# Paired matmuls on the parts of the array: inner products, chunk outputs and first low-rank factors of an RWKV-7 scan

## The chip, the cores and the metric

The kernel runs on one core of one Trainium2 chip, in one launch. The metric is the device time in microseconds (us) of one execution. The core's engines each work through their own list of instructions in order: PE (TensorE, matrix products into PSUM), DVE (VectorE), ACT (ScalarE), POOL (GpSimd) and SP, which here only starts transfers (DMA). An instruction waits where data or a buffer of another engine isn't there yet, and everything behind it on its engine waits too.

## The reference, cut to what matters

A net of several blocks on 1024 tokens of 1024 features, float32. The change is in one of them, the RWKV-7 time mix with 16 heads of 64 features:

```python
xs = x[None] + xx[None] * mu[:, None, None, :]          # six token-shift mixes
xr, xw, xk, xv, xa, xg = xs
r, k, v = jnp.einsum('nbtd,nde->nbte', jnp.stack([xr, xk, xv]), w_rkv)
w = -jax.nn.softplus(-(w0 + jnp.tanh(xw @ w1) @ w2)) - 0.5
a = jax.nn.sigmoid(a0 + (xa @ a1) @ a2)
g = jax.nn.sigmoid(xg @ g1) @ g2
...
def step(S, inp):                                       # one token, all heads
    r_t, w_t, k_t, v_t, a_t, b_t = inp
    sa = jnp.einsum('bhvk,bhk->bhv', S, a_t)
    S = S * w_t[:, :, None, :] + sa[..., None] * b_t[:, :, None, :] + v_t[..., None] * k_t[:, :, None, :]
    y = jnp.einsum('bhvk,bhk->bhv', S, r_t)
    return S, y
```

`w1` and `a1` are 1024 x 64, `g1` is 1024 x 160. The blocks ahead of it (a recurrent mixer, an FFN, an embedding) and behind it (output projection, FFN, embedding, a second net) aren't touched.

## The kernel before, in words

The time mix has two parts that are woven together on all engines.

The **dense part** (`rwkv_dense`) goes over four segments of 256 tokens. A segment has 28 units; a unit is one PSUM tile `mm` and eight steps over the features, each taking one mixed input (`M`, in 13 slots) and one slice of a 128-column weight tile. First come 8 units for v, then the four first low-rank factors (`low`), then 8 for r and 8 for k. The r, k and v units take three matmuls per step on operands split in two (L249 to L251 in the helper `mm3`); the four low-rank ones take one plain float32 matmul (L885). `w1` and `a1` are loaded side by side as the columns 0 to 63 and 64 to 127 of one tile, `both`; the unit of mix 1 and the unit of mix 4 each load that tile, each multiply all 128 columns, and each keep only their own 64 rows of the result. Mixes are made by ACT and DVE, weights come by DMA from the ACT queue, and split weights take ACT (L861) and DVE (L863). `finish` makes the scan's operands of a segment, and a chunk of 64 tokens can enter the scan when its segment's are in DRAM.

The **scan** (`rwkv_scan`) goes over 16 chunks of 64 tokens; the two heads of a pair lie on partitions 0 to 63 and 64 to 127. For each chunk: `inner` makes the products inside the chunk (tile `AM`, three slots, so that chunk c waits for the output of chunk c - 3), four pairs at a time from one load `BK`; their diagonal blocks go through DRAM to DVE, which inverts them by substitution (L1146, L1149), and back (L1157, L1168); `chain` carries the state (L1244, L1247, L1255, L1264); `outs` makes the chunk's output y for four pairs at a time (L1289 with the state, L1291 with the chunk's own tokens); `post` normalizes. `rwkv_out` projects the outputs of chunks that are done (tile `XO`).

A planner, `weave_`, sets the order of the instructions on every engine before the launch: tasks are generators that yield steps with an engine, a duration, waits and PSUM banks, and it issues next the step that a rough clock of the engines would start first. The durations in the steps only set that order. PSUM has 3 banks for the tag `g` (inner products, second factors and small products), 2 for `mm`, 2 for `ch`, 1 for `y`.

A float32 matmul stands in the trace as two records, so 8 records are 4 matmuls. In `inner` a matmul has 64 rows and 128 columns of the array, in L1289 64 by 64, in L1291 128 by 64, and elsewhere mostly 128 by 128; the trace writes that in front of the operand (`64*128`).

Of the kernel before, what the change touches and what calls it, by code (L numbers as in the profile page):

```python
# [10 lines left out]
AF = mybir.ActivationFunctionType  # L11
# [3 lines left out]
P = 128  # L15
# [41 lines left out]
class Net:  # L57
    """Feature-major activations: tile [128 features, 512 tokens] per (k, half)."""
# [16 lines left out]
    def open_group(self, T, W, S, L, psum):  # L75
        """Pools of one part of the net: T and S slots of [128, 516], weight slots, PSUM banks per tag."""
        self.close_group()
        self.bigx = ExitStack()
        self.nT = T
        self.big = self.bigx.enter_context(self.tc.tile_pool(name="big", bufs=1, reuse_waits="tile"))  # L80
        self.open_work(W, S, L, psum)

    def open_work(self, W, S, L, psum):
        """All of them but T anew."""
# [8 lines left out]
    def open_top(self):  # L93
        """One more pool above the group's, closed before them."""
# [4 lines left out]
    def open_rtop(self):  # L99
        """Another one, from the other end of the memory."""  # L100
# [44 lines left out]
    def s(self, dt=F32, n=HT):  # L145
        """scratch [128, n <= 516]"""
# [3 lines left out]
    def extra(self, tag, shape, dt, every, bufs):  # L150
        """now and then a slot of the pool on the right, where that is for more of the others"""
# [7 lines left out]
    def ld(self, src=None, n=HT, rows=P):  # L159
        """tile for a load; loads have slots of their own, for they run ahead"""  # L160
# [66 lines left out]
    def load_ws(self, srcs, nk, m, tag="w"):  # L227
        """srcs: DRAM APs arranged [p, nk, n] for columns c..c+n; returns hi, lo tiles [P, nk, m]"""
# [17 lines left out]
    def mm3(self, ps, w, x, first, last):  # L246
        """ps += w.T @ x with w = (hi, lo), x = (hi, lo)"""
# [5 lines left out]
    # W columns [c0, c0+128) for all nk row tiles  # L253
# [3 lines left out]
    def lin(self, w, xs, nk):  # L257
        """xs: list of (hi, lo) per k -> PSUM tile"""
# [6 lines left out]
    def rstd_bcast(self, acc, scale, eps, acc2=None):  # L265
        """acc [128, 512] -> PSUM [128, 512]: (sum over partitions * scale + eps)^-0.5 on all partitions; with acc2,
        for which that is the factor of another norm: that one and the product of both"""
# [34 lines left out]
    def square(self, h, k, half, gain=None):  # L302
        """h[k][half] is final: its part of the sum of squares (and of that of the products with the gain)"""
# [60 lines left out]
    def blocks(self, nblk, units, in_unit, post, nk_out, wout, h, add_bias=None, lag=2, delay=3, mid=None, late=None, fill=None, nlate=LATE):  # L364
        """units: weight items per block; in_unit(b, i, half, w) ; post(b, half) -> list of nk_out (hi, lo)"""
# [51 lines left out]
        # the first half of the last block before the second half of the one before it  # L417
# [34 lines left out]
    def hawk(self, h, xn, mid, late):  # L452
# [5 lines left out]
        # c8 = 8 softplus(-lam), softplus(z) = max(z, 0) + log1p(exp(-|z|)), log1p(e) = 2 atanh(e / (2 + e))  # L458
# [100 lines left out]
    def ple_prep(self, layer):  # L559
        """p, features on the partitions, split"""  # L560
# [40 lines left out]
    NSEG, SN = 4, 256  # token segments of the dense part  # L601

    def rwkv_consts(self):
# [7 lines left out]
        # block-diagonal ones (2 heads), identity minus the same / 64, and per-head selector columns  # L611
# [8 lines left out]
        # [s, t] masks on both heads: s < t | s <= t  # L620
# [19 lines left out]
        # operands of the scan, one chunk of 64 tokens after another  # L640
        self.qD, self.bkD, self.gbD = (d((16, P, KD, 2, 64), nm) for nm in ("qD", "bkD", "gbD"))
        self.vD = d((16, P, KD, 64), "vD")
        # second factors of the low-rank parts, for one pair after another
# [5 lines left out]
        # per head pair the decays between chunk middles; at the segments' ends in two factors  # L649
# [1636 lines left out]
```

## Time and profile before

| | |
|---|---|
| runs | 4188.85 us median of 3 (4186.73, 4188.85, 4215.79) |
| profiled execution | span 4186.6 us from the first to the last instruction; the page gives no other time for it |
| PE busy | 3949.4 us, 94% of the span |
| DVE, ACT, POOL busy | 61%, 35%, 4% |
| mean granted TensorE clock | 0.957 |
| woven stretch, dense part and scan | about 1340 to 2400 us |

The span of the profiled execution is within 0.1 us of the fastest run, so sums against it are sums against the runs. A busy PE is not PE at its peak: its matmuls are pipelined, so what a group costs is read from the starts of neighbouring instructions, not from their durations. PEclk is the granted clock as a share of 2.4 GHz; 0.5 is 1.2 GHz.

### The profile page before, as it was taken

How to read it: one execution, taken by the hardware profiler on the slowest of the kernel's cores; microseconds unless marked ns; L12 is line 12 of the kernel's file. 1: busy time of each engine (PE TensorE's matmuls, PEld its weight loads, DVE VectorE, ACT ScalarE, POOL GpSimd, SP SyncE). 2: the span in 40 equal slices, each digit the busy share in tenths (PEclk: the TensorE clock that was granted, in tenths of full speed). 3: DMA queues.
4: the chain of work that ended last, by engine and by line, in shares of the span. 5: the costliest groups of instructions: out<-in, count | busy, mean ns of one | idle time of the engine just before them, and what ended most of it. 6: DMA issues, size and time to landing. Idle time of an engine off the chain costs nothing.

```text
span 4186.6 us, 58441 instructions
## 1 busy us (share of the span) xinstructions
PE 3949.4 (94%) x22510; PEld 3216.6 (77%) x22510; DVE 2544.7 (61%) x5192; ACT 1466.1 (35%) x2491; POOL 179.3 (4%) x376
## 2 busy tenths in 40 slices
PE   6998999999988999999999699999999999999899
PEld 5776788888877877777867587888887877888687
DVE  6665733333364678777756476354536599997655
ACT  4455511111132665554542241111113332222533
POOL 0000000000000000000000101010100000000000
PEclk8999999999998999989979799999999999999999
DMA  3111111111122789676776541212211244332775
GB/s 103 48 47 34 51 46 51 41 56 51 34 67 88 216 252 237 174 209 170 194 194 173 97 127 52 63 49 66 63 49 58 71 119 118 109 115 96 236 226 186
DMA packets 695830, 464.49 MB, mean 111 GB/s; under 512 B 197956, under 2 KB 620800, under 8 KB 695552
## 3 DMA queue, kind: packets, MB, share of 16 engines
q1 hardware_dynamic: 514272, 367.80, 30.0%
q10 hardware_dynamic: 175872, 83.90, 7.3%
q0 software_dynamic: 5408, 9.06, 1.1%
q8 instruction: 177, 2.90, 0.3%
q14 instruction: 101, 0.83, 0.1%
HBM read 355.51 MB, written 106.69 MB: 110 GB/s over the span
## 4 chain that ended last, share of the span: by engine, by line
PE 69%; DVE 12%; DMA 7%; ACT 5%; issue 4%; SPq 1%; POOL 1%; ACTq 0%; DVEq 0%; POOLq 0%
PE mm L249 15%; PE mm L251 14%; PE mm L250 14%; PE ob L249 4%; PE ob L250 4%; PE ob L251 4%; DVE cy L1882 3%; PE g L1100 2%; PE g L926 1%; PE g L1438 1%; PE y L1291 1%; DMA BK<-bkD 1%; PE y L1289 1%; DVE w L863 1%; PE mm L2073 1%
## 5 line engine op out<-in xcount | busy, mean ns | idle before, releaser
L249 PE MATMUL mm<-T,w 128*128 128x512 f32 (+1 forms) x2944 | 1152.6, 393 | 47.1 <-ACT w L215 22.5
L251 PE MATMUL mm<-T,w 128*128 128x512 f32 (+1 forms) x2944 | 1149.9, 391 | 9.6 <-DVE w L216 9.6
L250 PE MATMUL mm<-T,w 128*128 128x512 f32 (+1 forms) x2944 | 1150.3, 392 | 1.1 <-DVE T L1380 0.9
L249 PEld LDWEIGHTS mm<-T,w 128*128 128x128 f32 x2944 | 558.6, 190 | 174.3 <-ACT w L215 26.9
L251 PEld LDWEIGHTS mm<-T,w 128*128 128x128 f32 x2944 | 559.0, 190 | 126.8 <-DVE w L216 12.1
L250 PEld LDWEIGHTS mm<-T,w 128*128 128x128 f32 x2944 | 559.7, 190 | 117.5 <-DVE T L1380 1.7
L215 ACT CAST w<-wraw 128x1024 fp32r<-128x1024 f32 (+1 forms) x286 | 288.4, 1014 | 988.8 <-PE mm L250 700.2
L216 DVE TENSOR_TENSOR w<-wraw,w 128x1024 fp32r<-128x1024 f32 (+1 forms) x286 | 335.1, 1177 | 373.9 <-ACT w L215 371.1
L389 DVE TENSOR_TENSOR h<-ob,h 128x512 f32<-128x512 f32 x416 | 286.1, 690 | 230.7 <-PE ob L251 227.5
L249 PE MATMUL ob<-S,w 128*128 128x512 f32 x896 | 359.2, 401 | 21.7 <-DVE h L389 21.1
L1882 DVE SCALAR_TENSOR_TENSOR cy<-cu,pv,cy 128x512 f32<-128x512 f32 x480 | 350.9, 749 | 12.3 <-ACT cy L1880 2.6
L250 PE MATMUL ob<-S,w 128*128 128x512 f32 x896 | 354.7, 396 | 0.2 <-DVE S L216 0.2
L251 PE MATMUL ob<-S,w 128*128 128x512 f32 x896 | 354.7, 396 | 0.0
L249 PE MATMUL mm<-M,w 128*128 128x256 f32 x768 | 255.1, 332 | 16.4 <-ACT M L837 8.5
L250 PE MATMUL mm<-N,w 128*128 128x256 f32 x768 | 229.7, 299 | 4.4 <-DVE N L839 4.3
L251 PE MATMUL mm<-M,w 128*128 128x256 f32 x768 | 229.8, 299 | 4.3 <-DVE w L863 4.0
L249 PEld LDWEIGHTS ob<-S,w 128*128 128x128 f32 x896 | 169.9, 190 | 70.2 <-DVE h L389 30.2
L251 PEld LDWEIGHTS ob<-S,w 128*128 128x128 f32 x896 | 169.7, 189 | 38.6
L250 PEld LDWEIGHTS ob<-S,w 128*128 128x128 f32 x896 | 170.1, 190 | 36.3 <-DVE S L216 0.6
L249 PEld LDWEIGHTS mm<-M,w 128*128 128x128 f32 x768 | 157.0, 204 | 50.3 <-issue 23.3
L439 DVE TENSOR_TENSOR S<-mm,S 128x512 f32<-128x512 f32 x88 | 60.8, 690 | 211.7 <-PE mm L251 209.8
L215 ACT CAST S<-S 128x512 fp32r<-128x512 f32 x128 | 79.3, 620 | 266.3 <-DVE S L439 154.4
(458 smaller groups left out, 5431.9 us busy)
## 6 DMA issues: line engine op xcount, KB each, us to landing
wraw<-in_rw_w_rkv_dram ACTq DMA_DIRECT2D x96, 512.0 KB
wraw<-in_ffn_w_in_dram SPq DMA_DIRECT2D x88, 512.0 KB
wraw<-in_w_in_dram SPq DMA_DIRECT2D x48, 512.0 KB
wraw<-in_ffn_w_out_dram SPq DMA_DIRECT2D x44, 512.0 KB
BK<-bkD SPq DMA_DIRECT2D x64, 256.0 KB
wraw<-in_rw_w_o_dram ACTq DMA_DIRECT2D x24, 512.0 KB
wraw<-in_lru_w_in_dram SPq DMA_DIRECT2D x20, 512.0 KB
wraw<-in_ple_w_gate_dram SPq DMA_DIRECT2D x16, 512.0 KB
```

Source lines behind the costliest of these rows:

```text
L215: self.nc.scalar.copy(hi, x)
L216: self.nc.vector.tensor_sub(lo, x, hi.bitcast(F32))
L249: nc.tensor.matmul(ps, w[0], x[0], start=first, stop=False)
L250: nc.tensor.matmul(ps, w[0], x[1], start=False, stop=False)
L251: nc.tensor.matmul(ps, w[1], x[0], start=False, stop=last)
L389: nc.vector.tensor_add(h[m][half], ps, h[m][half])
L439: nc.vector.tensor_mul(a, ps, sg.pop((b, j, half)))
L863: nc.vector.tensor_sub(wl.rearrange(fl), r.rearrange(fl), wh.bitcast(F32).rearrange(fl))
L926: nc.tensor.matmul(ps, lw[r0:r1, slot, :], HW[hx][r0:r1], start=x == 0, stop=x == len(rows) - 1)
L1100: nc.tensor.matmul(g[:, 128 * x : 128 * x + 128], bk[rs, x].rearrange("p a b -> p (a b)"), qt[rs, j0 + x].rearrange("p a b -> p (a b)"), s ...
L1289: nc.tensor.matmul(o[rs], s[rs, x], qz[rs, j, 1, :], start=True, stop=False)
L1882: nc.vector.scalar_tensor_tensor(y, x[:, k : k + HT], cw(k), y, ALU.mult, ALU.add)
```

## The change

Three edits, and what follows from them.

1. **Inner products.** The two heads' matmuls of a half chunk are written in turn, into two banks of tag `g` that are both taken before the first of them; the two masked copies on DVE come behind all eight.
2. **Chunk outputs.** The eight products with the state come first, then the eight with the chunk's own tokens. The step's written duration is 1.2 for 1.3.
3. **First factors.** The units of mix 1 and mix 4 become one unit with one load of `both`: for every feature slice one matmul of 64 columns for mix 1 and one for mix 4, in turn, into the two halves of one PSUM tile. Their mixes are made in turn, two by two. A segment has 27 units for 28, and 16 matmuls of 128 x 64 for 16 of 128 x 128.

Comments and docstrings are dropped too, which moves the line numbers. The core of the diff:

```diff
+        rsl = [slice(0, 64), slice(64, P)]
...
         both = [(self.wcols(W1, 0, KD, 64), 0, 64), (self.wcols(A1, 0, KD, 64), 64, 64)]
-        low = [(1, both, (AF.Tanh, 0, 64, 0)), (4, both, (AF.Copy, 64, 128, 0)),
+        low = [((1, 4), both, ((AF.Tanh, 0, 64, 0), (AF.Copy, 64, 128, 0))),
                (5, w128(G1, 0), (AF.Sigmoid, 0, 128, 1)), (5, w128(G1, 32), (AF.Sigmoid, 96, 128, 2))]
...
         order = []
         for u in units:
-            if (u[0], 0) not in order:
+            if isinstance(u[0], tuple):
+                order += [(i, k + y) for k in range(0, KD, 2) for i in u[0] for y in range(2)]
+            elif (u[0], 0) not in order:
                 order += [(u[0], k) for k in range(KD)]
...
-            exact = lambda x: str(units[jobs[x][1]][0]) in EX[jobs[x][0]]
+            exact = lambda x: isinstance(units[jobs[x][1]][0], tuple) or str(units[jobs[x][1]][0]) in EX[jobs[x][0]]
...
+                if isinstance(i, tuple):
+                    w = W.pop(x)
+                    for k in range(0, KD, 2):
+                        end = k == KD - 2
+                        sig = [("p", x)] * end + [("free", freed + y) for y in range(4)]
+                        wait = [("mix", seg, z, k + y) for z in i for y in range(2)] + [("w", x)] * (k == 0)
+                        ps = yield E("P", 1.74 * f, lat=0.15 if end else 0.0, wait=wait, sig=sig, bank=None if k else "mm")
+                        if k == 0:
+                            PSU[x] = ps
+                        freed += 4
+                        for y in range(2):
+                            for z, c in zip(i, rsl):
+                                nc.tensor.matmul(PSU[x][c, 0:n], w[:, k + y, c], M.pop((seg, z, k + y)),
+                                                 start=k + y == 0, stop=k + y == KD - 1)
+                    continue
...
-                if len(what) == 2:
+                if isinstance(what[0], tuple):
+                    if seg:
+                        w += [("fin", seg - 1, j) for j in range(KD)]
+                    for func, r0, r1, slot in what:
+                        yield E("A", AE, wait=w, rel=(lambda: PSU[x]) if r1 == P else None, sig=[("u", x)] if r1 == P else [])
+                        if r0 == 0:
+                            HW[slot] = top(f"HW{slot}", (P, n), 1)
+                        nc.scalar.activation(HW[slot][r0:r1], PSU[x][r0:r1, 0:n], func)
+                    PSU.pop(x)
+                elif len(what) == 2:
...
-                    for hd, rs in enumerate(rsl):
-                        x = 2 * c + j0 // 4
-                        g = yield E("P", 0.87, bank="g", use=0.5, wait=own(c) + past(c - NAM if c < NT else -1) + [("q", c), ("bk", x), "xn"],
-                                    sig=[("bf", x)] if hd else ())
-                        am, bk, qt = AM(c), BK[x], QT(c)
-                        for x in range(4):
+                    x = 2 * c + j0 // 4
+                    gs = [(yield E("P", 0.0, lat=0.0, bank="g", wait=own(c) + past(c - NAM if c < NT else -1) + [("q", c), ("bk", x), "xn"]))]
+                    gs.append((yield E("P", 1.0, bank="g", sig=[("bf", x)])))
+                    am, bk, qt = AM(c), BK[x], QT(c)
+                    for x in range(4):
+                        for g, rs in zip(gs, rsl):
                             nc.tensor.matmul(g[:, 128 * x : 128 * x + 128],
                                              bk[rs, x].rearrange("p a b -> p (a b)"),
                                              qt[rs, j0 + x].rearrange("p a b -> p (a b)"), start=True, stop=True)
+                    for hd, g in enumerate(gs):
                         yield E("V", 0.6, rel=g, par=not (j0 and hd), sig=[("am", c)] if j0 and hd else ())
                         nc.vector.tensor_mul(am[:, j0 : j0 + 4, hd].rearrange("p c a b -> p c (a b)"),
                                              g.rearrange("p (c x) -> p c x", c=4), mask)
...
-                y = yield E("P", 1.3 if c else 0.62, bank="y", use=0.6, wait=[("S", c, h)])
+                y = yield E("P", 1.2 if c else 0.62, bank="y", use=0.6, wait=[("S", c, h)])
                 s = st[h][c]
+
+                for x in range(4) if c else ():
+                    for rs in rsl:
+                        nc.tensor.matmul(y[rs, 64 * x : 64 * x + 64], s[rs, x], qz[rs, 4 * h + x, 1, :],
+                                         start=x == 0, stop=False, skip_group_check=True)
                 for x in range(4):
-                    j = 4 * h + x
-                    o = y[:, 64 * x : 64 * x + 64]
-                    if c:
-                        for hd, rs in enumerate(rsl):
-                            nc.tensor.matmul(o[rs], s[rs, x], qz[rs, j, 1, :], start=True, stop=False)
                     for hd, rs in enumerate(rsl):
-                        nc.tensor.matmul(o[rs], uv[:, j, hd, :], am[:, j, hd, 1, :], start=not c, stop=True)
+                        nc.tensor.matmul(y[rs, 64 * x : 64 * x + 64], uv[:, 4 * h + x, hd, :], am[:, 4 * h + x, hd, 1, :],
+                                         start=not c and x == 0, stop=x == 3, skip_group_check=True)
                 yield E("A", 0.26, rel=y, wait=[("out", c - 2)] if c >= 2 else [], sig=[("y", c, h)])
                 nc.scalar.copy(PY[c % 2][:, 256 * h : 256 * h + 256], y[:, 0:256])
...
-                  (net.reopen([("u", net.NSEG * 28 - 1)], ["rtop"], True), 0.0)]
+                  (net.reopen([("u", net.NSEG * 27 - 1)], ["rtop"], True), 0.0)]
```

What this does to the order on PE, at three places. The number behind a name is the buffer; `x4` counts matmuls.

Inner products of the first chunk on PE, before (g: PSUM bank, QT and BK: operands; L249 to L251: a k or r unit):

```order
L249 MATMUL mm_11296<-M_10969,w_11265 128x256
L250 MATMUL mm_11296<-N_10970,w_11265 128x256
L251 MATMUL mm_11296<-M_10969,w_11266 128x256
L1100 MATMUL g_11313<-QT_8758,BK_10536 128x128 x4
L249 MATMUL mm_11296<-M_10986,w_11265 128x256
L250 MATMUL mm_11296<-N_10987,w_11265 128x256
L251 MATMUL mm_11296<-M_10986,w_11266 128x256
L1100 MATMUL g_11323<-QT_8758,BK_10536 128x128 x4
L249 MATMUL mm_11296<-M_10996,w_11265 128x256
L250 MATMUL mm_11296<-N_10997,w_11265 128x256
```

and now:

```order
L249 MATMUL mm_11288<-M_10959,w_11258 128x256
L250 MATMUL mm_11288<-N_10960,w_11258 128x256
L251 MATMUL mm_11288<-M_10959,w_11259 128x256
L1125 MATMUL g_11305<-QT_8758,BK_10513 128x128
L1125 MATMUL g_11306<-QT_8758,BK_10513 128x128
L1125 MATMUL g_11305<-QT_8758,BK_10513 128x128
L1125 MATMUL g_11306<-QT_8758,BK_10513 128x128
L1125 MATMUL g_11305<-QT_8758,BK_10513 128x128
L1125 MATMUL g_11306<-QT_8758,BK_10513 128x128
L1125 MATMUL g_11305<-QT_8758,BK_10513 128x128
L1125 MATMUL g_11306<-QT_8758,BK_10513 128x128
L249 MATMUL mm_11288<-M_10976,w_11258 128x256
```

Two stays of four matmuls on one head each, with three matmuls of a full-size unit between them, became one stay of eight that changes bank at every matmul.

Chunk outputs on PE (QT, St: with the state; AM, UV: own tokens), chunk 1 before:

```order
L251 MATMUL mm_13395<-M_13085,w_13193 128x256
L1289 MATMUL y_13592<-QT_8759,St_13312 64x64 x2
L1291 MATMUL y_13592<-AM_11470,UV_8766 64x64 x2
L1289 MATMUL y_13592<-QT_8759,St_13312 64x64 x2
L1291 MATMUL y_13592<-AM_11470,UV_8766 64x64 x2
L1289 MATMUL y_13592<-QT_8759,St_13312 64x64 x2
L1291 MATMUL y_13592<-AM_11470,UV_8766 64x64 x2
L1289 MATMUL y_13592<-QT_8759,St_13312 64x64 x2
L1291 MATMUL y_13592<-AM_11470,UV_8766 64x64 x2
L1179 MATMUL g_13614<-XT_13583,AM_11667 32x32 x16
```

and now, the same chunk:

```order
L904 MATMUL mm_13246<-M_12905,wraw_12571 128x256
L1313 MATMUL y_13312<-QT_8759,St_13043 64x64 x8
L1317 MATMUL y_13312<-AM_11458,UV_8766 64x64 x8
L904 MATMUL mm_13246<-M_12919,wraw_12571 128x256
L1125 MATMUL g_13343<-QT_8758,BK_11924 128x128
```

The two kinds, which took turns by pairs, stand as eight and eight; before and behind them stand other units as ever.

First factors of the first segment on PE, at the border of the two units before (wraw: the weight tile, loaded twice):

```order
L885 MATMUL mm_9167<-M_9135,wraw_9053 128x256
L885 MATMUL mm_9167<-M_9140,wraw_9053 128x256
L885 MATMUL mm_9167<-M_9150,wraw_9053 128x256
L885 MATMUL mm_9200<-M_9155,wraw_9088 128x256
L885 MATMUL mm_9200<-M_9165,wraw_9088 128x256
L885 MATMUL mm_9200<-M_9172,wraw_9088 128x256
L885 MATMUL mm_9200<-M_9176,wraw_9088 128x256
```

and now, at the start of the one unit:

```order
L250 MATMUL mm_9126<-N_8898,w_9096 128x256
L251 MATMUL mm_9126<-M_8897,w_9097 128x256
L886 MATMUL mm_9166<-M_8893,wraw_9053 64x256
L886 MATMUL mm_9166<-M_8900,wraw_9053 64x256
L886 MATMUL mm_9166<-M_8910,wraw_9053 64x256
L886 MATMUL mm_9166<-M_8925,wraw_9053 64x256
L886 MATMUL mm_9166<-M_8917,wraw_9053 64x256
L886 MATMUL mm_9166<-M_9139,wraw_9053 64x256
```

The sixteen matmuls stay sixteen but have half the columns, all read one weight tile and write one PSUM tile. All told, between the first projection matmul and the last chunk's output, the order on PE has 806 places before where the array's tile form changes between neighbouring matmuls and 606 now. Runs of first-factor matmuls on PE are 29 before; now they are 8 of the new unit (16 | 4, 8, 4 | 4, 4, 4, 4 | 16 matmuls) and 25 of the other two. The scan's last chunk keeps its place: its inner products stand behind 10 or 11 of the 16 output-projection tiles of the tail before and now.

## Rows read from the trace of the kernel before

**Rows 1.** The page's head: span, then busy time of PE.
```profile
span 4186.6 us, 58441 instructions
PE 3949.4 (94%) x22510; PEld 3216.6 (77%) x22510; DVE 2544.7 (61%) x5192; ACT 1466.1 (35%) x2491; POOL 179.3 (4%) x376
```

**Rows 2.** Windows of the woven stretch: length, busy PE PEld DVE ACT POOL, clock, DMA share, GB/s.
```profile
1340.00:1700.00 360.00, 327.54 (x2145) 276.44 (x2146) 260.45 (x640) 227.38 (x499) 22.00 (x70) 0.92 0.83 227
1700.00:2160.00 460.00, 446.12 (x5176) 362.01 (x5177) 333.55 (x1101) 234.29 (x536) 35.81 (x84) 0.92 0.69 184
2160.00:2345.00 185.00, 167.65 (x1730) 134.89 (x1726) 110.75 (x359) 53.90 (x102) 14.34 (x19) 0.88 0.64 170
2345.00:2410.00 65.00, 28.00 (x218) 21.11 (x219) 21.25 (x37) 17.11 (x32) 3.30 (x5) 0.50 0.50 105
...
1871.00:1898.00 27.00, 26.07 (x137) 20.85 (x137) 15.28 (x45) 8.53 (x20) 2.40 (x5) 0.50 0.64 175
```

**Rows 3.** Timeline of PE, inner products: start, busy; the last row at half clock.
```profile
1571.76 0.28 PE L250 MATMUL mm<-N,w 128*128 128x256 f32 x1
1571.88 0.28 PE L251 MATMUL mm<-M,w 128*128 128x256 f32 x1
1572.09 1.16 PE L1100 MATMUL g<-QT,BK 64*128 64x128 f32 x8
1573.18 0.39 PE L249 MATMUL mm<-M,w 128*128 128x256 f32 x1
1573.40 0.28 PE L250 MATMUL mm<-N,w 128*128 128x256 f32 x1
...
1884.23 2.07 PE L1100 MATMUL g<-QT,BK 64*128 64x128 f32 x8
```

**Rows 4.** Timeline of PE, chain products and outputs of the first chunk.
```profile
1712.37 0.28 PE L1244 MATMUL ch<-UV,AM 64*64 64x64 f32 x4
1712.49 0.28 PE L1247 MATMUL ch<-St,QT 64*64 64x64 f32 x4
...
1713.72 0.69 PE L1291 MATMUL y<-AM,UV 128*64 128x64 f32 x16
1714.33 0.69 PE L1189 MATMUL g<-YF,WL 32*32 32x32 f32 x32
```

**Rows 5.** Windows of line L1100 alone: PE and PEld busy, records.
```profile
1340.00:2160.00 820.00, 58.77 (x384) 49.32 (x384) 0.92 0.75 203
2160.00:2400.00 240.00, 21.21 (x128) 17.87 (x128) 0.79 0.60 152
```

**Rows 6.** Timeline of PE, outputs of a later chunk.
```profile
1862.65 0.33 PE L1289 MATMUL y<-QT,St 64*64 64x64 f32 x4
1862.91 0.34 PE L1291 MATMUL y<-AM,UV 128*64 128x64 f32 x4
1863.18 0.33 PE L1289 MATMUL y<-QT,St 64*64 64x64 f32 x4
...
1864.76 0.39 PE L249 MATMUL mm<-M,w 128*128 128x256 f32 x1
```

**Rows 7.** Windows of line L1289 alone.
```profile
1340.00:2160.00 820.00, 26.46 (x320) 15.56 (x320) 0.92 0.75 203
2160.00:2400.00 240.00, 15.57 (x160) 9.39 (x160) 0.79 0.60 152
```

**Rows 8.** Timeline of PE, the four low-rank units of the first segment.
```profile
1383.63 13.98 PE L885 MATMUL mm<-M,wraw 128*128 128x256 f32 x64
```

**Rows 9.** The chain of waits between 1520 and 1560: start, length, what.
```profile
1527.56 11.15 DMA wraw<-in_rw_w_rkv_dram
```

**Rows 10.** Timeline of PE at the end of the scan.
```profile
2367.25 0.31 PE L1179 MATMUL g<-XT,AM 32*32 32x32 f32 x2 [26.58 <-DVE XT L1173]
```

**Rows 11.** The chain of waits between 2270 and 2400.
```profile
2340.65 6.70 SPq L1157
...
2358.47 6.37 DMA yiD<-YB
```

More of the change, by code (lines that the diff above doesn't have):

```diff
@@ L910, in evac @@
                         w += [("fin", seg - 1, j) for j in range(KD)]
-                    yield E("A", AE, wait=w, rel=lambda: PSU[x], sig=[] if func == AF.Sigmoid else [("u", x)])
+                    yield E("A", AE, wait=w, rel=lambda: PSU[x])
                     ps = PSU.pop(x)[:, 0:n]
-                    if slot == 0 and r0 == 0 or slot:
-                        HW[slot] = top(f"HW{slot}", (P, n), 1)
+                    HW[slot] = top(f"HW{slot}", (P, n), 1)
                     o = HW[slot]
-                    if func == AF.Sigmoid:
-                        nc.scalar.activation(o[r0:r1], ps[r0:r1], AF.Tanh, scale=0.5)
-                        yield E("A", AE, sig=[("u", x)])
-                        nc.scalar.activation(o[r0:r1], o[r0:r1], AF.Copy, bias=0.5, scale=0.5)
-                    else:
-                        nc.scalar.activation(o[r0:r1], ps[r0:r1], func)
+                    nc.scalar.activation(o[r0:r1], ps[r0:r1], AF.Tanh, scale=0.5)
+                    yield E("A", AE, sig=[("u", x)])
+                    nc.scalar.activation(o[r0:r1], o[r0:r1], AF.Copy, bias=0.5, scale=0.5)
         def lora2(ps, lw, rows):
```

## The prediction, as it was put on record

> **What bounds the kernel now.** First the head of the page: PE is busy 94% of the span [rows 1]. The change lies in the woven stretch, so I read that in windows [rows 2]. From 1340 to 1700 us PE is busy 327.5 of 360 us (91%), with the DMA engines at 83%; from 1700 to 2160 it is busy 446.1 of 460 us (97%), with DVE at 73% and ACT at 51%. There PE's list of instructions sets the pace, and time taken out of it should shorten the stretch. From 2160 to 2345 the scan's last four chunks run beside the output projection (PE 91%), and from 2345 to 2410 PE is busy 28 of 65 us at half the clock: it has nothing left to fill with and waits 26.58 us for the transpose of the last inverse [rows 10]. On the chain there stand SP's issues of the inverse's stores and their transfer, the first of them 6.70 us and the transfer 6.37 us [rows 11]. That end is latency, not PE.
>
> Then the timeline of PE, for what the touched groups cost. Busy times overlap, so I go by starts. Full-size matmuls start 0.12 us apart (1571.76, 1571.88) [rows 3].
>
> **Inner products.** From the last full-size matmul before a stay of four (1571.88) to the second behind it (1573.40) are 1.52 us [rows 3]; less two full-size ones at 0.12 a stay costs 1.28 us. There are 64 stays, 512 records of 8 each, 48 of them before 2160 [rows 5]. After, 32 stays of eight matmuls. If the two heads run beside each other on the upper and lower half of the array, a stay lasts as long as one does now, and 1.28 us go per half chunk: 24 x 1.28 = 31 us before 2160, 8 x 1.28 = 10 behind. No row shows two matmuls of 64 rows and 128 columns side by side, so I bound it. A float32 matmul is two records, so one of 256 columns takes 13.98 / 32 = 0.44 us [rows 8], one of 128 takes 0.22 and four take 0.87; a stay of eight in sequence would be 1.28 + 0.87 = 2.15, and only the second entry and exit would go: 2.56 - 2.15 = 0.41 us, 10 us before 2160 and 3 behind. The nearest rows are the chain's products of 64 by 64, whose groups of two matmuls start 0.12 us apart (1712.37, 1712.49) [rows 4], about the time of one (64 columns: 0.44 / 4 = 0.11). They sit on the same two row halves, so I take the full 31 and 10.
>
> The Trainium skill, TensorEngine Tiling (Array Packing), Gotcha 1: PSUM Pressure, says that different row tiles write to different banks and can't access the same bank at once; the two banks of the new order would fulfil that, and no row here shows it. The skill's TensorE: Matmul & The Clock Gate, Measured speedup vs the span model, gives 3.07 and not 4 for four row tiles; an estimate from that page for two is 1.54, by which a stay would be 0.41 + 1.74 / 1.54 = 1.54 us, the saving before 2160 24 us for 31, and the time some 5 us longer than mine.
>
> The stay of eight holds two of the three `g` banks until two masked copies are done, where before the second bank was taken one stay later. Behind it on PE may stand a second factor or a small product that wants a `g` bank. The cover is the projection matmuls that stand between; I cost it at nothing and let it count in what doesn't arrive.
>
> **Chunk outputs.** A later chunk's step for four pairs goes from 1862.65 to 1864.76, 2.11 us, in eight groups 0.26 us apart [rows 6]. A group of two matmuls of one form costs 0.12 where the form stays [rows 4]; so 0.14 of each group is the change of form, and the sort takes six or seven of eight changes away. The first chunk has only the own-token products, 8 matmuls in one piece: 1713.72 to 1714.33, 0.61 us [rows 4]. Two such pieces are 1.22, so 0.89 us go per step. There are 320 records of L1289, 16 to a step, before 2160 and 160 behind [rows 7]: 20 x 0.89 = 18 us and 10 x 0.89 = 9 us. The lower bound is zero, if the 0.26 were the operands' own time; the 0.61 speaks against it.
>
> **First factors.** The two units are 16 matmuls of 0.44 us in each of four segments, 28 us [rows 8]. With 64 columns of weights for each, pairs fit side by side; the piece of 0.61 us holds 8 matmuls of this very form (128 by 64) that would take 8 x 0.11 = 0.87 one after the other [rows 4], so such pairs do run side by side. That gives 14 us; the lower bound is none. The order enters the new form in eight runs, and an entry and exit cost 1.28 - 0.87 = 0.41 us at most: up to 3 us back. I take 12. One load of 512 KB in 28 per segment falls away, in a stretch where a weight transfer of 11.15 us stands on the chain [rows 9]. Against that, 16 mixes are now eaten in half the time: the unit can find its mixes not made yet, since 8 of 13 slots hold v's until v's last unit. All of this lies before 2160.
>
> **Sum.** 31 + 18 + 12 = 61 us of PE time go before 2160, 10 + 9 = 19 behind. How much arrives is my choice: three quarters of the 61, 46 us, since for 46 us of that stretch (6%) PE already waits, mostly in its DMA-heavy first part [rows 2], and a faster PE waits more for weights and mixes of ACT and DVE. Behind 2160 I count only what stands on the last chunks' way, inner products and outputs of the chunks 12 and 15: 4 x 1.28 + 4 x 0.89 = 8.7, and of it half, 4 us. The rest of the 19 only lengthens the wait of 26.58 us. So 50 us: 4186.6 - 50 = 4137 us in the profiled execution; the median of the runs lies 2 us over its span, so **4138 us**.
>
> **The rivals.**
>
> *All of it arrives*, with the clock a little better. The granted clock is 0.92 up to 2160 [rows 2], which is 2 x 0.08 x 820 = 131 us at 1.2 GHz. I choose 30 of these as what denser stays could save, which gives 15 us. Then 61 + 10 + 15 = 86: 4103. For it speaks the 97% of the second window, against it the waits of the first.
>
> *The heads don't run beside each other*: 10 + 18 + 12 = 40, three quarters 30, behind 2160 some 3: 4156. This is the case in which the largest edit doesn't do what it says.
>
> *The time turns into waits.* The unit of first factors waits for mixes, the stays for two banks, the faster units for DMA at 83% [rows 2, 9]. With 30% arriving: 18 + 2 = 20: 4169.
>
> *Slower: the clock.* PE that finishes sooner idles more between its pieces, and in the emptier tail the clock was 0.50 [rows 2]. At half the clock the same stay takes 2.07 for 1.16 us [rows 3], so each microsecond there loses about half. The stretch from 1871 to 1898 shows that it can fall with PE busy 26 of 27 us, amid small products [rows 2]. To eat the 50 us it takes 100 us more at 1.2 GHz than the 131; from there on the kernel is slower. At 140 more: 4207. Against it: the change takes 200 places out of the order where the array's form changes, and leaves the large matmuls.
>
> **Chances and range.** Forecast 0.45, all arrives 0.15, heads in sequence 0.12, waits 0.20, clock 0.08. The forecast's own range, from half to all of the 61, is 4120 to 4155. The range that holds 8 in 10 is **4105 to 4175**: it leaves out the better half of the second case, the clock and a little of the waits. About 1%, 42 us, is what a measurement of this kernel tells from no change: faster than 4147 are nearly all of the forecast and all of the second case, with a little of the third, 0.57; within 1% the rest of these, the waits and most of the clock, 0.39; slower 0.04.
>
> **What would show it.** In the changed trace a stay of inner products should be 16 records whose neighbours in the order start a few ns apart in pairs, some 1.1 us from first start to the next matmul; 1.95 would mean heads in sequence. A chunk's output should go in two pieces of 0.6 us, the new unit's 16 matmuls in about 3.6 us where they stand together; gaps ahead of them with DVE or ACT as releaser are the mixes. The dense part's last matmul should come some 45 us sooner, at the same clock, and the wait ahead of the last transpose stay at 20 to 35 us. I am wrong if the windows up to 2160 show PE below 90%, a granted clock under 0.88, or if the tail grows by what the dense part gave.

## The result, and the profile after

The changed kernel takes 4131.8 us (median of 4 runs, 4126.11 to 4148.83), the kernel before 4187.8 (4 runs, 4175.52 to 4215.79): a ratio of 0.9857 [0.9818, 0.9897], 56 us or 1.4% faster. The profiled executions span 4128.9 and 4186.6 us, 57.7 apart.

The head of the changed kernel's page answers to [rows 1].

```profile
span 4128.9 us, 58410 instructions
PE 3866.6 (94%) x22510; PEld 3141.8 (76%) x22510; DVE 2537.3 (61%) x5192; ACT 1463.1 (35%) x2491; POOL 183.3 (4%) x376
```

PE's 22510 matmul records take 82.8 us less; DVE and ACT are as they were.

The windows, with columns as in [rows 2], but cut where the last second factor ends: 2156.0 us before, 2120.1 after.

```profile
1340.00:1700.00 360.00, 320.58 (x2328) 261.50 (x2328) 259.13 (x642) 225.59 (x500) 20.70 (x70) 0.91 0.79 217
1700.00:2120.00 420.00, 397.83 (x5088) 322.34 (x5087) 329.49 (x1092) 231.81 (x532) 40.94 (x84) 0.95 0.75 202
2120.00:2299.00 179.00, 145.83 (x1633) 117.74 (x1632) 109.61 (x369) 55.18 (x103) 14.44 (x19) 0.87 0.68 181
2299.00:2350.00 51.00, 21.58 (x216) 17.46 (x217) 20.67 (x34) 16.46 (x32) 3.29 (x5) 0.57 0.55 120
```

Up to there PE is busy 718.4 of 780 us, where it was 770.3 of 816. Up to the last dense projection matmul (the first mark below) it is busy 695.8 of 756.0 us, where it was 753.2 of 797.1: 57.4 us less work and 16.3 us more waiting, so 41 us arrive. The clock of 0.91 and 0.95 makes 2 x (0.09 x 360 + 0.05 x 420) = 107 us at 1.2 GHz, where it was 131.

Two marks fix where the 57.7 us lie: the group line of L250 on the mix's low half, whose last start is the last dense projection matmul, and that of the outputs' second product. Columns: records, least, median and greatest ns, first and last start. First the kernel before, then the changed one.

```profile
L250 PE MATMUL mm<-N,w x768: 274/282/583, 1352.7 to 2137.1; 128*128 128x256 f32 x192
L1291 PE MATMUL y<-AM,UV x512: 222/270/369, 1713.7 to 2380.8; 128*64 128x64 f32 x171
```

```profile
L250 PE MATMUL mm<-N,w x768: 276/282/582, 1352.5 to 2096.0; 128*128 128x256 f32 x192
L1317 PE MATMUL y<-AM,UV x512: 221/222/367, 1697.3 to 2323.8; 128*64 128x64 f32 x171
```

The dense part ends 41 us sooner and the scan's last output 57. So about 41 us come from the dense part and 16 from the tail; behind the last output nothing changes (1805 us to the end in both).

Timeline of PE in the changed kernel, start and busy: a stay of inner products [rows 3], the outputs of one chunk [rows 6], the new unit of first factors with one of the other units [rows 8].

```profile
1566.58 0.28 PE L251 MATMUL mm<-M,w 128*128 128x256 f32 x1
1566.79 1.16 PE L1125 MATMUL g<-QT,BK 64*128 64x128 f32 x16
1567.88 0.39 PE L249 MATMUL mm<-M,w 128*128 128x256 f32 x1
1568.10 0.28 PE L250 MATMUL mm<-N,w 128*128 128x256 f32 x1
...
2010.28 0.68 PE L1313 MATMUL y<-QT,St 64*64 64x64 f32 x16
2010.89 0.69 PE L1317 MATMUL y<-AM,UV 128*64 128x64 f32 x16
2011.50 0.39 PE L249 MATMUL mm<-M,w 128*128 128x256 f32 x1
...
1383.16 3.91 PE L886 MATMUL mm<-M,wraw 128*64 128x256 f32 x26
1387.22 1.08 PE L886 MATMUL mm<-M,wraw 128*64 128x256 f32 x6 [0.15 <-DVE M L831]
1388.23 7.63 PE L904 MATMUL mm<-M,wraw 128*128 128x256 f32 x32
```

- From the full-size matmul ahead of the stay (1566.58) to the second behind it (1568.10) are 1.52 us, the very number of [rows 3], with 16 records in place of 8: the two heads run beside each other.
- A chunk's outputs take 1.22 us (2010.28 to 2011.50), not 2.11.
- The first factors' 16 matmuls take 5.07 us (1383.16 to 1388.23) where I gave 3.6. The idle times ahead of the new unit's matmuls and weight loads say why (us, times), from the view of line L886; below them a row of DVE's timeline, which makes the mixes:

```profile
its engine sat idle before it (us, times) until:
  DVE M L831: 6.9, 16
  issue: 2.2, 8
...
1384.93 3.43 DVE L831 SCALAR_TENSOR_TENSOR M<-X,omu,M 128x256 f32<-128x256 f32 x8 [0.18 <-ACT M L829]
```

TensorE waits 16 times for a mix of DVE's, 13 times ahead of a weight load (5.9 us) and 3 times ahead of a matmul (1.0 us). Before, the same view of L885 has 11 such waits with 3.2 us, over twice as many records. In the row of 1384.93 DVE makes a mix in 3.43 / 8 = 0.43 us, and a pair of matmuls eats two of them in about that time (3.6 / 8 = 0.45 us by the forecast). By starts the four units cost 23.4 us, of which 4 us were at half the clock. The two units that they replace cost 28 us in the prediction's estimate (16 x 0.44 us in each of four segments): some 5 us saved.

The tail, timeline of PE. First the last chunk's four inner-product stays in the kernel before, then its two in the changed kernel with the wait that answers to [rows 10].

```profile
2275.06 2.07 PE L1100 MATMUL g<-QT,BK 64*128 64x128 f32 x8
2279.64 2.07 PE L1100 MATMUL g<-QT,BK 64*128 64x128 f32 x8
2291.73 1.16 PE L1100 MATMUL g<-QT,BK 64*128 64x128 f32 x8
2301.75 1.16 PE L1100 MATMUL g<-QT,BK 64*128 64x128 f32 x8
```

```profile
2243.44 1.16 PE L1125 MATMUL g<-QT,BK 64*128 64x128 f32 x16
2249.46 1.16 PE L1125 MATMUL g<-QT,BK 64*128 64x128 f32 x16
2313.72 0.28 PE L1205 MATMUL g<-XT,AM 32*32 32x32 f32 x2 [24.48 <-DVE XT L1199]
```

Before, the order spread them over 27.8 us (2275.06 to 2302.9), other work between and two of them at half the clock. Now they are done in 7.2 us, and everything behind them starts sooner. The wait for the last transpose stays: 24.48 us for 26.58. So does the end's latency on the chain of waits [rows 11]:

```profile
2288.43 4.15 SPq L1183
...
2292.62 4.39 SPq L1183
...
2297.06 1.28 SPq L1183
...
2298.39 13.01 DMA yiD<-YB
```

They run from 2288.43 to 2311.40: 23.0 us. Before, the four pieces that answer to these, of which [rows 11] show the first and the last, ran from 2340.65 to 2364.84: 24.2 us.

### The profile page after: what moved, and what is told of

Its sections match the earlier page's. It is cut to its first block, busy times and chain, and to the rows that moved or that the text cites. A ratio compares the mean times of both kernels' runs of the same rounds, so it can differ in the third digit from the quotient of the medians.

```text
span 4128.9 us, 58410 instructions
## 1 busy us (share of the span) xinstructions
PE 3866.6 (94%) x22510; PEld 3141.8 (76%) x22510; DVE 2537.3 (61%) x5192; ACT 1463.1 (35%) x2491; POOL 183.3 (4%) x376
## 4 chain that ended last, share of the span: by engine, by line
PE 38%; DVE 9%; DMA 8%; issue 3%; ACT 1%; SPq 1%; POOL 0%; ACTq 0%; POOLq 0%; DVEq 0%
PE mm L249 8%; PE mm L251 8%; PE mm L250 8%; DVE cy L1909 3%; PE ob L249 2%; PE ob L251 2%; PE ob L250 2%; PE g L950 1%; DMA YF<-yiD 1%; DMA yiD<-YB 1%; PE mm L2098 1%; PE mm L2100 1%; PE mm L2099 1%; DMA GB<-abD 1%; DMA wraw<-in_w_in_dram 1%
## 5 line engine op out<-in xcount | busy, mean ns | idle before, releaser
L249 PE MATMUL mm<-T,w 128*128 128x512 f32 (+1 forms) x2944 | 1153.5, 393 | 46.3 <-ACT w L215 22.7
L251 PE MATMUL mm<-T,w 128*128 128x512 f32 (+1 forms) x2944 | 1150.8, 392 | 8.8 <-DVE w L216 8.8
L250 PE MATMUL mm<-T,w 128*128 128x512 f32 (+1 forms) x2944 | 1149.7, 391 | 1.0 <-DVE T L1407 0.9
L249 PEld LDWEIGHTS mm<-T,w 128*128 128x128 f32 x2944 | 559.4, 190 | 173.5 <-ACT w L215 27.1
L251 PEld LDWEIGHTS mm<-T,w 128*128 128x128 f32 x2944 | 559.6, 190 | 126.4 <-DVE w L216 11.8
L250 PEld LDWEIGHTS mm<-T,w 128*128 128x128 f32 x2944 | 560.0, 190 | 117.0 <-DVE T L1407 1.8
L249 PE MATMUL ob<-S,w 128*128 128x512 f32 x896 | 359.0, 401 | 22.5 <-DVE h L389 22.0
L251 PE MATMUL ob<-S,w 128*128 128x512 f32 x896 | 354.4, 396 | 0.0
L250 PE MATMUL ob<-S,w 128*128 128x512 f32 x896 | 354.3, 395 | 0.1
L249 PE MATMUL mm<-M,w 128*128 128x256 f32 x768 | 252.0, 328 | 12.8 <-ACT M L841 10.0
L250 PE MATMUL mm<-N,w 128*128 128x256 f32 x768 | 226.7, 295 | 4.0 <-DVE N L843 3.9
L251 PE MATMUL mm<-M,w 128*128 128x256 f32 x768 | 226.0, 294 | 4.0 <-DVE w L867 4.0
L249 PEld LDWEIGHTS ob<-S,w 128*128 128x128 f32 x896 | 169.8, 190 | 71.1 <-DVE h L389 31.4
L251 PEld LDWEIGHTS ob<-S,w 128*128 128x128 f32 x896 | 169.6, 189 | 38.5
L250 PEld LDWEIGHTS ob<-S,w 128*128 128x128 f32 x896 | 170.0, 190 | 36.3 <-DVE S L216 0.6
L249 PEld LDWEIGHTS mm<-M,w 128*128 128x128 f32 x768 | 153.0, 199 | 46.3 <-issue 22.9
```

What stands on the lines that cost most here:

```text
L249: nc.tensor.matmul(ps, w[0], x[0], start=first, stop=False)
L250: nc.tensor.matmul(ps, w[0], x[1], start=False, stop=False)
L251: nc.tensor.matmul(ps, w[1], x[0], start=False, stop=last)
```

## The experiments

All are ratios to the kernel before, with 95% intervals; the changed kernel's is that of the result, the others come from five rounds each. In the expectations Theory A is the mechanism of the prediction, C the plan of the order, D the planner's number, M the mixes, E the place of the output projection. The differences against the changed kernel are ratio differences times 4190 us. Those below about 20 us don't clear the two intervals taken together, so of the kernels made from the changed one only a_outs_turn clears them, and barely. I read the others together with the marks of the traces, one profiled execution each: last start in the dense part, last output, span.

| kernel | ratio [95%] | dense end | last output | span |
|---|---|---|---|---|
| before | 1 | 2137.1 | 2380.8 | 4186.6 |
| changed | 0.9857 [0.9818, 0.9897] | 2096.0 | 2323.8 | 4128.9 |
| a_inner_seq | 0.9889 [0.9861, 0.9917] | 2095.0 | 2334.8 | 4142.9 |
| a_outs_turn | 0.9914 [0.9884, 0.9945] | 2090.9 | 2336.6 | 4142.9 |
| a_inner_use05 | 0.9894 [0.9866, 0.9923] | 2089.2 | 2336.8 | 4141.4 |
| a_no_low | 0.9857 [0.9830, 0.9884] | 2085.1 | 2322.8 | 4131.0 |
| b_inner | 0.9906 [0.9873, 0.9938] | 2101.6 | 2339.7 | 4146.5 |
| b_outs_sorted | 0.9936 [0.9916, 0.9956] | 2124.8 | 2368.0 | 4168.8 |
| b_low | 0.9997 [0.9976, 1.0017] | 2151.2 | 2381.5 | 4193.8 |
| b_inner_use1 | 1.0032 [1.0006, 1.0057] | 2164.7 | 2400.2 | 4210.4 |
| a_lora_pair | 0.9890 [0.9865, 0.9914] | 2058.2 | 2274.2 | 4151.1 |
| a_lora_pair_out | 0.9902 [0.9874, 0.9930] | 2062.1 | 2333.2 | 4154.8 |
| a_lora_pair_use05 | 0.9880 [0.9851, 0.9909] | 2075.7 | 2328.8 | 4139.3 |

### One part undone in the changed kernel

**a_inner_seq**: the stay's eight matmuls head by head, nothing else moved.

```diff
-for x in range(4):
-    for g, rs in zip(gs, rsl):
+for g, rs in zip(gs, rsl):
+    for x in range(4):
```

> The changed kernel with one thing undone: inside a stay of inner products the four matmuls of the first head come first and then the four of the second, into the same two banks; the order on DVE, ACT, POOL and SP stays the same, and on PE only these eight matmuls change places. Theory A (the heads run beside each other): a stay goes from 1.09 us (after's trace) to about 1.96 (4 x 0.22 more), 24 stays of 32 lie in the dense part, so its end moves back by 0.87 x 24 = 21 us of PE time, of which some 15 arrive; whole kernel about 15 to 20 us over the changed one, 4145 to 4150. Rival B (only the second entry and exit mattered): stays stay near 1.1 us and the time does not move, 4129. Rival C (the gain came from the new plan of the order, since the plan is the same here): the stay gets longer, but the time moves by under 5 us.

Timeline of PE of this kernel, a stay and what is behind it:

```profile
1565.27 1.68 PE L1125 MATMUL g<-QT,BK 64*128 64x128 f32 x16 [0.77 <-DMA BK<-bkD]
1566.88 0.38 PE L249 MATMUL mm<-M,w 128*128 128x256 f32 x1
```

The stay takes 1.61 us here (1.64 typically) and not 1.09: only the order of eight matmuls differs, so the turn-taking is what pays, 0.55 us a stay. But it isn't 1.96 either. In the trace the second head's first matmul starts right behind the first head's fifth record of eight (1565.80 us; the first head's last record, the one that signals its bank, starts at 1566.13): PE overlaps the row halves by three records even when they are written in sequence. The ratio gives 13 us over the changed kernel, the span 14, and 24 x 0.55 is 13 for the stays of the dense part. By the ratio alone rival C isn't excluded; the span and the last output, 11 us later, speak against it. Yet the last dense matmul comes when it did (2095.0 for 2096.0). What took the loss up ahead of there is PE's waiting: up to 2095 us PE is busy 704.5 of 755 us, in the changed kernel 694.8 of the same 755. Chunk 12's inner products, the first work of the tail, already start 6.9 us later (2146.6 for 2139.7).

**a_outs_turn**: the output loops of before, state product and own-token product in turn, in the changed kernel.

```diff
-for x in range(4) if c else ():       # all four state products
-    ...
-for x in range(4):                    # all own-token products
-    ...
+for x in range(4):
+    if c: ...                         # this pair's state product
+    ...                               # this pair's own-token product
```

> The changed kernel with the chunk outputs in turn again by pairs (two products with the state, two with the own tokens), and the plan of the order left as it is. Theory A (a change of the array's form costs 0.14 us): a step goes from 1.23 back to 2.11 us, 20 steps before the dense part's end, 18 us of PE time, of which three quarters arrive, and some 2 to 5 us on the last chunks' way: 4143 to 4150. Rival C (the plan made the gain): under 5 us.

The groups are 0.26 us apart again, a chunk's step 2.11 us. The ratio says 24 us slower than the changed kernel, the span 14. Rival C, under 5 us, is out by that, though the intervals leave little room. Its dense part spent less time at half the clock than the changed kernel's (65 us for 99, summed from the trace between 1340 us and the last dense matmul), which hides some of its price in this one execution.

**a_no_low**: the changed kernel with the first factors as they were, two units of 128 by 128.

> The changed kernel with the first factors as they were (two units of 128 columns, 28 loads a segment); inner products in turn and outputs sorted stay. Theory M (the fused unit waits for its mixes, and alone it moved the kernel by a ratio of 0.9997): the same time as the changed kernel within 8 us, 4124 to 4140 where before takes 4190. Theory A as forecast: 9 us slower than the changed kernel.

No difference: 0.9857, spans 4131.0 and 4128.9. The dense part even ends 11 us sooner without that edit, and the tail loses the 11 us again.

**a_inner_use05**: the second bank of the pair is planned at half its time, which changes the order alone.

```diff
-gs.append((yield E("P", 1.0, bank="g", sig=[("bf", x)])))
+gs.append((yield E("P", 1.0, bank="g", use=0.5, sig=[("bf", x)])))
```

> The changed kernel with the planner told that a stay of inner products fills half of the array (use=0.5, as before the change), not all of it; the matmuls are the same, only the order of the steps changes. In the changed trace the last chunk's inner products take 7 us (2244.6 to 2251.9) where they took 26 (2277.2 to 2303.6), and this shortened the scan's end by some 16 us more than forecast. Theory D (the planner's weight did that, since a step of over 0.9 gets a bonus against other PE work while the clock is low): the last chunk's inner products spread again to over 15 us, and the time goes up by 10 to 19 us, 4139 to 4148. Rival (the shorter stay itself did it): they stay under 10 us and the time within 6 us of the changed kernel's.

The last chunk's two stays, timeline of PE:

```profile
2247.86 1.16 PE L1125 MATMUL g<-QT,BK 64*128 64x128 f32 x16
...
2261.84 1.16 PE L1125 MATMUL g<-QT,BK 64*128 64x128 f32 x16
```

They spread over 15.1 us again (7.2), and from the start of chunk 12's inner products to the end of the last output it takes 192.8 us, not 184.3 (before: 201.7). The ratio says 15 us slower than the changed kernel, the span 12. So with this one number about half of the tail's unexpected gain goes back. That the place of the last stays did it is argued and not shown: in a_outs_turn they lie as close as in the changed kernel (7.2 us), and its tail takes 191.3 us all the same.

### One part alone in the kernel before

**b_inner** takes the new inner products, **b_outs_sorted** the two sorted output loops, **b_low** the unit of first factors.

> The kernel before with the inner-product edit alone (heads in turn, two banks, one step that the planner counts as the whole array). Theory A: 64 stays of 1.09 us become 32 of 1.09, some 31 us of PE time less before the dense part's end, 23 of it arriving, and with the last chunk's inner products drawn together another 10 to 17 in the tail: 30 to 40 us under the kernel before. If only the dense part gains (no effect of the planner's weight on the tail): 20 to 25 us. If the edits are worth the same time whatever stands beside them, this and the parts of the others add up to the 56 us of the whole change.

> The kernel before with one part of the change: the chunk outputs sorted by kind, with the planner's duration left at 1.3, so that the order of everything else stays as it was. Theory A: a step goes from 2.11 to 1.23 us, 18 us less PE time in the dense part, of which some 13 arrive, and 2 to 4 in the tail: 13 to 17 us under the kernel before. Rival (PE's freed time turns into waits, because the order was planned for the old lengths): under 6 us.

> The kernel before with the fused unit of first factors alone. Theory A as forecast: 12 us of PE time less before the dense part's end, 9 arriving. Theory M (the mixes aren't ready, since in the changed trace the unit's 16 matmuls, written in one piece, take 5.1 and 5.9 us from start to the next matmul and not 3.6): about half, 3 to 6 us, and the waits ahead of its matmuls name DVE or ACT. Either way within 12 us of the kernel before.

Inner products give 39 us, outputs 27, first factors nothing (1, interval -7 to 10). The three sum to 0.0161, the whole change gave 0.0143, so within the intervals the parts add. b_inner has 36 of the 40 us of its span by the end of the dense part; my price was 31 us of PE time there and 10 behind. That is more than all of the PE time: in this execution the dense part also had 79 us at half the clock for 116, worth some 19 us if work takes twice as long there (an estimate, by the 2.07 us for 1.16 of [rows 3]). b_outs_sorted: 18 us in the span for 27 in the ratio; 13 of the 18 are there at the last output, and the rest lies behind it, where nothing was changed. With the fused unit the dense part ends later in both pairs of traces, 14 us here (2151.2 for 2137.1) and 11 us in the changed kernel against a_no_low, and the last output comes at the same time within 1 us; why is open.

**b_inner_use1** leaves the four stays of before as they are, but plans their bank at full time: the planner's number alone.

```diff
-g = yield E("P", 0.87, bank="g", use=0.5, wait=own(c) ...
+g = yield E("P", 0.87, bank="g", wait=own(c) ...
```

> The kernel before with the planner's number alone: the steps of the inner products are given as filling the whole array (no use=0.5), the matmuls are as before, 64 stays. Theory D (the weight draws the last chunk's inner products together): they take under 12 us instead of 27.8 (2275.1 to 2302.9), the stretch from the last segment's first inner products to the last output shrinks by some 10 us from 201.7, and the kernel is 5 to 12 us faster. Rival (the shorter stay did it): the last chunk's stay spread over 20 us or more, and the time is within 5 us of before.

The last chunk draws together (18.5 us for 27.8) and the tail falls from 201.7 to 196.0 us, but the dense part ends 28 us later, with 153 us at half the clock (116 in the kernel before, summed as above), and the whole is 13 us slower, where Theory D had 5 to 12 us faster. So the planner's number alone isn't the gain.

### The same idea once more

**a_lora_pair** puts the two second factors of 64 rows side by side into two banks, as the heads are.

```diff
-pz = yield E("P", 0.87 * f, wait=[("fl", x_)], bank="g", use=0.5)
+pz = yield E("P", 0.0, lat=0.0, wait=[("fl", x_)], bank="g")
+pa = yield E("P", 1.0 * f, bank="g")
+zw = lora2(pz, lw, [(0, 0, 0, 64)])
+za = lora2(pa, lw, [(0, 0, 64, 128)])
...                                   # the old step for za, further down, goes
```

> The changed kernel with one more pair: the second factors of w and a (64 rows each, upper and lower half of the array, 128 columns, 256 moving) are computed as one step into two banks g, as the inner products are. In the changed trace one of them costs 0.63 us from its start to the next matmul; two of them stand apart 32 times. Theory A: as a pair they cost 0.63 plus some ns once, so 32 x 0.63 = 20 us of PE time less, nearly all before the dense part's end, some 12 to 15 us arriving: about 13 us under the changed kernel. Rival (the dense part is by now held by DVE, ACT and DMA): within 5 us of it. Rival (two of the three g banks held at once): slower by a few us.

Timeline of PE of this kernel, a pair and, from another unit, a single one:

```profile
1445.54 0.70 PE L950 MATMUL g<-HW,l 64*128 64x256 f32 x4
...
1590.49 0.70 PE L950 MATMUL g<-HW,l 64*128 64x256 f32 x2 [1.98 <-DVE AM L1130]
```

Four records are as long as two: side by side again. The dense part ends 38 us sooner than in the changed kernel, and the last output comes 50 us sooner, yet the end comes 14 to 22 us later. Not all of the 38 us is the pair's: chunk 12's inner products start 21 us sooner (2118.9 for 2139.7), about the 20 us of PE time that were forecast. Windows of the tile XO on PE, the output projection: length, PE busy (records), clock, DMA share, GB/s; first this kernel, then the changed one.

```profile
2100.00:2200.00 100.00, 7.42 (x15) 0.76 0.55 156
2200.00:2290.00 90.00, 38.44 (x120) 0.90 0.67 130
2290.00:2350.00 60.00, 44.51 (x249) 0.84 0.47 141
```

```profile
2100.00:2200.00 100.00, 40.95 (x150) 0.81 0.80 230
2200.00:2290.00 90.00, 43.63 (x236) 0.94 0.54 144
2290.00:2350.00 60.00, 0.00 (x0) 0.57 0.59 104
```

Two thirds of the output projection (249 records) now run behind the last output, where nothing covers them; in the changed kernel all are done by 2290. They come late because their loads do, on SP's queue:

```profile
2115.09 0.32 SPq L1399 DMA_DIRECT2D XR<-outD  x1
...
2207.09 0.32 SPq L1399 DMA_DIRECT2D XR<-outD  x1
```

The order places one load at 2115 and the next 92 us later, while PE is busy only 65.65 of 100 us.

**a_lora_pair_out** asks the planner to prefer the output projection (a bonus of 2.0), **a_lora_pair_use05** plans the second bank at half its time.

> The changed kernel with the paired second factors of the run before (dense part and scan ended 50 us sooner there, at 2274 against 2324 us for the last output, and the whole was 20 us slower, since 249 of 384 matmul records of the output projection stood behind the scan's end), and with a bonus of 2.0 us for the planner's output projection tasks, by which all 384 stand ahead of the last chunk's state product again. Theory E (the projection's place ate the gain): the last output comes at some 2285 to 2310 and the kernel takes 15 to 35 us less than the changed one, ratio to before about 0.978 to 0.982. Rival (scan and projection need the same time, whatever the order, since PE has no more idle time there): within 8 us of the changed kernel.

> The changed kernel with the paired second factors, and the planner told that this step fills half of the array; the order then has 339 of 384 records of the output projection ahead of the last chunk's state product and 45 behind. Theory E: some 5 to 25 us less than the changed kernel, ratio to before 0.980 to 0.985. Rival: within 8 us of it.

With the bonus, 369 of 384 records lie at 2215 to 2303, ahead of the last output, but that comes at 2333 instead of 2274: what the projection gained the scan's chain lost. With half the time, 273 lie at 2182 to 2295 and 96 behind a gap of 18 us. Both ratios lie by the first one's, 19 and 10 us over the changed kernel's, so Theory E failed twice: to move the projection didn't bring the 50 us to the end. That projection and scan share what PE time the tail has would fit this, but it isn't shown; the rival said so too, and had the times within 8 us of the changed kernel. No version here beats the changed kernel; a_no_low equals it with one edit less.

Pairs of both heads in one bank would have spared the second bank. That was not tried.

## Why the prediction was right, step by step

The forecast of 4138 us lay 6 us over the median, a gain of 50 us against 56. The costs of its two big groups were read rightly. Two smaller terms were off in opposite directions: the first factors brought the kernel nothing for the 9 us that were to arrive of 12, the tail 16 us for 4. That the total came this close is in part luck. One sign of being wrong did show: from 1340 to 1700 us PE is busy 320.6 of 360 us, 89.0% and so under the 90% of the prediction. The other two, a clock under 0.88 up to there and a longer tail, did not.

- **Inner products, 1.28 us a stay**: right. Two stays became one of the same length, by [rows 3] and the row of 1566.79; a_inner_seq shows that the stay's length comes from taking the heads in turn. The estimate from the Trainium skill (TensorE: Matmul & The Clock Gate, Measured speedup vs the span model), 1.54 us for a stay, is refuted for this case by 1.28, counted the same way (1.52 less two full-size ones at 0.12).
- **Chunk outputs, 2.11 to 1.22**: right to the hundredth. The prediction let three quarters of the 18 us arrive and half of the tail's 4 x 0.89, some 15 us; b_outs_sorted gives 13 (at the last output) to 27 us (by the ratio), a_outs_turn 14 to 24.
- **First factors, 12 us**: failed. The pairs do run side by side, but "16 mixes are now eaten in half the time: the unit can find its mixes not made yet" is what happens, 16 waits with 6.9 us, and of 12 us about 5 remain in PE's time. The order also enters the new form nine times, by the list of runs ahead of the prediction, and not eight. For the kernel b_low and a_no_low measure nothing. I named these waits and did not price them.
- **Three quarters arrive by the end of the dense part, 46 us**: 41. With the first factors at 5, PE's pieces there shrink by 31 + 18 + 5 = 54 us. Its busy time fell by 57, and 16 us more of waiting leave 41. No idle time ahead of the stays is put down to the masked copies that free a bank, so the wait for two banks shows no cost. Up to that mark there are 17 us less at half the clock (99 for 116), which should add some 8 to the 54; I can't place the 5 us that are then too many. That three quarters arrive was a choice, and it held for the whole only: b_inner alone has 36 us by that mark, b_low -14.
- **Tail, 4 us**: mis-sized, it gave 16. I priced what stands on the chain's way as PE time, 8.7 us and half of it. I did not count that the order stretched the last chunk's four stays over 27.8 us and now sets two in 7.2. By a_inner_use05 about half of the tail's gain goes back with one planner's number; by b_inner_use1 that number without the shorter stays gives only 5.7 us there; by a_outs_turn the outputs in turn take 7.0 us of it back with the stays as close as now. How the gain divides between stays, outputs and the order is open.
- **The end is latency**: right: 24.48 us of wait, and 23.0 us of issues and transfer where 24.2 were.
- **Rivals**: heads in sequence would have been 4156; a_inner_seq, which is that case in part, has 0.9889 of the kernel before, 4142 on the scale of the forecast. The clock went the other way, 107 us at 1.2 GHz for 131. That all arrives fell with the 16 us of waiting, the third rival with 41 of 57 us arriving.

## What to carry to other kernels

Sort small matmuls by the form of the array, and put the two row halves in turn into separate banks: here each gained by itself, 27 and 39 us, on a PE that is busy 94%. A fused unit gains only as much as its inputs keep up. Before counting freed PE time as time of the kernel, look for who must refill it: a_lora_pair reached the last output 50 us sooner and the end later, with the work that had filled the tail coming late.

## What the runs showed of the hardware

- In turn on the two row halves, two products of 64 rows and 128 columns cost nothing beyond one: a stay of eight matmuls takes 1.092 us, one of four 1.085 (medians at full clock, changed kernel and kernel before). The two of a pair start 6 to 7 ns apart. Second factors with 256 columns do the same in a_lora_pair (0.633 us for a pair, 0.626 for one in the changed kernel).
- PE starts matmuls of the other row half about three records ahead of their place in the list: in a_inner_seq four matmuls on one half and then four on the other take 1.64 us, where my expectation for that was 1.96. So on the row halves PE doesn't keep strictly to the order of its list.
- In the chunk outputs the two heads' products lie on different row halves and write the two partition halves of the one bank of `y`. They start 6 to 7 ns apart there too (line L1313).
- A change of form costs about 0.14 us: groups 0.26 us apart with it, 0.12 without. The Trainium skill, TensorEngine Tiling (Array Packing), Key Properties, has it that changing the tiling mode drains TensorE. The trace agrees in that a change costs time, with that number; whether it is a drain, no run here shows.
